# Low parts of split operands on VectorE instead of GpSimd, outside the DeltaNet's input projections

## The chip, the core and the metric

One core of a Trainium2 chip. The metric is device time in us of one execution of the kernel; the value for a kernel is the median of its runs. PE is TensorE (PEld its weight loads), DVE is VectorE, ACT is ScalarE, POOL is GpSimd, SP is SyncE, which issues most DMAs.

## What is computed

Two layers over 1040 positions (16 meta tokens and 1024 inputs) of width 1024, all in float32: the first with a gated DeltaNet as token mixer, the second with an mLSTM, each followed by a squared-ReLU MLP of width 4096.

```
for layer in range(DEPTH):                       # DEPTH = 2
    hn = rms_norm(h, attn_norm[layer])
    if layer == 0:
        mix = gated_deltanet(hn, gdn_in, gdn_conv, gdn_a_log, gdn_dt_bias, gdn_norm, gdn_out)
    else:
        mix = mlstm(hn, mlstm_in, mlstm_gate_bias, mlstm_norm, mlstm_out)
    h = h + mix
    h = h + squared_relu_mlp(rms_norm(h, ffn_norm[layer]), ff_up[layer], ff_down[layer])
return h[:, N_META:]

def squared_relu_mlp(h, w_up, w_down):
    a = jax.nn.relu(h @ w_up)
    return (a * a) @ w_down
```

The DeltaNet projects hn to queries, keys, values and gates (`gdn_in`, 6176 columns), runs a recurrence over chunks for 16 heads, and projects the result back (`gdn_out`). The mLSTM does the same with `mlstm_in` (3088 columns), 8 heads and `mlstm_out`.

## The kernel before

Every large matrix product is made from split operands. A float32 value x is written as hi + lo: hi is x rounded to the reduced-precision type that TensorE takes, made by a copy on ScalarE, and lo = x - hi, a subtraction of two SBUF tiles. `mm3` (lines 114 to 117) then issues three matmuls for each pair of tiles: hi weights with hi activations (line 115), hi weights with lo activations (116), lo weights with hi activations (117). A PSUM tile has up to 264 columns in the first layer and 504 in the last down projection.

Who makes the lo parts is the subject here:
- `load_split` (line 127) loads a block of weights into `wraw`, copies it to `whi` on ScalarE (line 134) and subtracts into `wlo` (line 135), on GpSimd unless the caller names another engine. No caller does. It is called 96 times for the DeltaNet's input projections (`GDN.load_w`), 32 for its output projection (`OutUnits.load_w`), 72 for the two down projections (`Down.tiles`), 28 for the mLSTM's input projections and 20 for its output (16 of them of 768 columns, the rest of all of 1024). Both `whi` and `wlo` have two buffers.
- `Norm.apply` (line 970 on) makes the mLSTM's normalised input; the lo parts of every second row block (8 of 16) are made by GpSimd (line 986).
- `Norm.combine` (line 989 on) makes the seven combinations of the up projection's input, for each half of the positions: 4 steps of three products and sums in SBUF (`st_b`, `st_t`, lines 1003 to 1008), then `xhi` on ScalarE and `xlo`, three of seven blocks on GpSimd (line 1011, 780 columns), four on VectorE (line 1013).
- `Up` is the up projection with seven products instead of eight for every 2 x 2 blocks (Strassen's scheme in Winograd's form). `Up.operand` makes one of the seven weight operands: sums of blocks on VectorE (line 1046), hi on ScalarE (1062), lo at line 1064. `Up.evac` adds the products up on VectorE (line 1075) and writes the activations to DRAM. A job has a flag `help`; where it is set, GpSimd makes the lo part of four of the seven operands. It is set in the first three jobs, which run on one half of the positions while `combine` still makes the other half, and in the last two, while the first activations for the down projection are loaded.

In the down projection `Down.load` splits activations on VectorE (line 1149), and each finished PSUM tile is added to the residual `hT` by VectorE (line 1168). In the DeltaNet's output projection that is line 917, from PSUM tiles with two buffers (`pj`); with it goes a square on ScalarE and its addition into `ss` on VectorE (line 941), for the next norm.

The order on each engine is set by the framework's scheduler, which takes the program's operations with their dependencies and its own estimate of their time. GpSimd also does small work of the DeltaNet and the mLSTM (powers, masks, copies), which the change leaves where it is.

Of the kernel before, what the change touches and what calls it, by code (L numbers as in the profile page):

```python
# [7 lines left out]
F32 = mybir.dt.float32  # L8
F32R = mybir.dt.float32r
AF = mybir.ActivationFunctionType  # L10
ALU = mybir.AluOpType
# [4 lines left out]
P = 128  # L16
D = 1024
KT = D // P
# [32 lines left out]
def pair(pool):  # L51
    return tuple(pool.tile([P, 2, HALF], F32R, tag=t, name="act_" + t) for t in ("hi", "lo"))
# [61 lines left out]
def mm3(nc, ps, whi, wlo, xhi, xlo, first, last):  # L114
    nc.tensor.matmul(ps, whi, xhi, start=first, stop=False)  # L115
    nc.tensor.matmul(ps, whi, xlo, start=False, stop=False)  # L116
    nc.tensor.matmul(ps, wlo, xhi, start=False, stop=last)  # L117


def staging(c, shape):  # L120
    n = 1
    for d in shape[1:]:
        n *= d
    raw = c.wraw.tile([P, 2 * HALF], F32, tag="wraw", name="wraw")[:, :n]
    return raw.rearrange("p (a b) -> p a b", a=shape[1]) if len(shape) == 3 else raw


def load_split(c, src, shape, lo_engine=None):
    nc = c.nc
    raw = staging(c, shape)  # L130
    nc.sync.dma_start(out=raw, in_=src)
    hi = c.whl.tile(shape, F32R, tag="whi", name="whi")
    lo = c.whl.tile(shape, F32R, tag="wlo", name="wlo")
    nc.scalar.copy(hi, raw)  # L134
    (lo_engine or nc.gpsimd).tensor_tensor(lo, raw, hi.bitcast(F32), op=ALU.subtract)  # L135
    return hi, lo


def rows_view(w):
    return w.rearrange("(k p) f -> p k f", p=P)  # L140
# [63 lines left out]
class GDN:  # L204
# [235 lines left out]
        yield  # L440

    def load_w(self, col):
        return load_split(self.c, rows_view(self.w)[:, :, col:col + P], [P, KT, P])

    def dense(self, whl, hf, g, m=P):
        c, n = self.c, GL[hf] // 2
# [399 lines left out]
class OutUnits:  # L846
# [17 lines left out]
    def load_w(self, k8, d):  # L864
        return load_split(self.c, rows_view(self.w)[:, 8 * k8:8 * k8 + 8, d * P:(d + 1) * P], [P, KT, P])
# [57 lines left out]
class Norm:  # L923
# [46 lines left out]
    def apply(self, hf, pool):  # L970

        nc, c = self.nc, self.c
        self.x[hf] = []
        yield
        yield
        r = yield from self.rms(hf)
        ts = slice(hf * HALF, (hf + 1) * HALF)
        for k in range(KT):
            xn = self.pool.tile([P, HALF], F32, tag="xn", name="nxn", bufs=2)
            nc.vector.scalar_tensor_tensor(xn, c.hT[:, k, ts], self.nw[:, k:k + 1],  # L980
                                           r.rearrange("p a b -> p (a b)"), op0=ALU.mult, op1=ALU.mult)
            if k % 2 == 0:
                self.x[hf].append(pair(pool))
            hi, lo = (x[:, k % 2] for x in self.x[hf][-1])
            nc.scalar.copy(hi, xn)
            (nc.vector, nc.gpsimd)[k % 2].tensor_tensor(lo, xn, hi.bitcast(F32), op=ALU.subtract)
            yield

    def combine(self, hf, pool):

        nc, c = self.nc, self.c
        self.x[hf] = []
        yield
        yield
        r = yield from self.rms(hf)
        ts = slice(hf * HALF, (hf + 1) * HALF)
        for j in range(KT // 2):
            b, t = (x.rearrange("p (a b) -> p a b", b=G) for x in self.stages())  # L1000
            hi, lo = (pool.tile([P, 7, G], F32R, tag=n, name=n) for n in ("xhi", "xlo"))
            for k, out in ((j, b[:, 0:4:3]), (j + 4, b[:, 1:3])):
                nc.vector.scalar_tensor_tensor(out, c.hT[:, k, ts].rearrange("p (a b) -> p a b", b=G),  # L1003
                                               self.nw[:, k:k + 1], r, op0=ALU.mult, op1=ALU.mult)
            nc.vector.tensor_tensor(t[:, 0], b[:, 3], b[:, 0], op=ALU.subtract)
            nc.vector.tensor_tensor(t[:, 2], b[:, 2], b[:, 3], op=ALU.subtract)
            nc.vector.tensor_tensor(t[:, 1], b[:, 2], t[:, 0], op=ALU.subtract)
            nc.vector.tensor_tensor(t[:, 3], b[:, 1], t[:, 1], op=ALU.subtract)  # L1008
            yield
            nc.scalar.copy(hi[:, 0:3], b[:, 0:3])  # L1010
            nc.gpsimd.tensor_tensor(lo[:, 0:3], b[:, 0:3], hi[:, 0:3].bitcast(F32), op=ALU.subtract)  # L1011
            nc.scalar.copy(hi[:, 3:7], t)
            nc.vector.tensor_tensor(lo[:, 3:7], t, hi[:, 3:7].bitcast(F32), op=ALU.subtract)
            self.x[hf].append((hi, lo))
            yield


class Up:
# [17 lines left out]
        nc.sync.dma_start(out=r2, in_=w[:, :, (2 * i + 1) * P:(2 * i + 2) * P])  # L1036
        return r1, r2

    def operand(self, raw, name, help):

        nc, c = self.nc, self.c
        r1, r2 = raw[:2]
        a11, a12, a21, a22 = r1[:, 0:4], r1[:, 4:8], r2[:, 0:4], r2[:, 4:8]

        def sub(out, a, b, op=ALU.subtract):
            nc.vector.tensor_tensor(out, a, b, op=op)  # L1046
            return out
        if name == "s2":
            s3 = self.u1.tile([P, KT // 2, P], F32, tag="s3", name="s3")
            raw.append(sub(s3, a11, a21))  # L1050
            x = sub(a11, a22, s3)
        elif name == "s3":
            x = raw[2]
        elif name == "s1":
            x = sub(a21, a21, a22, ALU.add)
        elif name == "s4":
            x = sub(a12, a12, a11)
        else:
            x = {"a11": a11, "a12": a12, "a22": a22}[name]
        w = c.whl.tile([P, KT, P], F32R, tag=("whi", "wlo")[self.nop % 2], name="uop")  # L1060
        self.nop += 1
        nc.scalar.copy(w[:, 0:4], x)  # L1062
        lo = nc.gpsimd if help and name in ("a12", "s3", "a22", "s4") else nc.vector
        lo.tensor_tensor(w[:, 4:8], x, w[:, 0:4].bitcast(F32), op=ALU.subtract)  # L1064
        return w

    def evac(self, i, hs, name, ps, tmp):
# [33 lines left out]
    def run(self, jobs):  # L1101

        n, ahead = len(self.ORDER), 3
        raws, ops = {0: list(self.load(jobs[0][0]))}, {}
        done = 0
        for ji, (i, parts, help, before) in enumerate(jobs):
            if before:
                before()
            hs = slice(parts[0], parts[-1] + 1)
            tmp = {}  # L1110
            for u, (name, xi) in enumerate(self.ORDER):
                while done <= min(ji * n + u + ahead, len(jobs) * n - 1):
                    dj, du = divmod(done, n)
                    ops[done] = self.operand(raws[dj], self.ORDER[du][0], jobs[dj][2])
                    if du == n - 1 and dj + 1 < len(jobs):
                        raws[dj + 1] = list(self.load(jobs[dj + 1][0]))
                    done += 1
                w = ops.pop(ji * n + u)
                ps = self.ps.tile([P, 2, 512], F32, tag="pu", name="ps_up")[:, :, :G]
                for hf in parts:  # L1120
                    for k in range(4):
                        hi, lo = (x[:, xi] for x in self.norm.x[hf][k])
                        mm3(self.nc, ps[:, hf], w[:, k], w[:, 4 + k], hi, lo, k == 0, k == 3)
                    yield
                self.evac(i, hs, name, ps[:, hs], tmp)
# [62 lines left out]
def mlp(c, w_up, w_down, norm, spans, sides, xa, st, acts, after, closed):  # L1188


    down = Down(c, w_down, acts, after, spans)
    n, e = FF // P // 2, 3
    c.norm_psum(False)
    with ExitStack() as ust:
        up = Up(c, w_up, norm, acts, ust, sides[1])
        c.bg.append(norm.combine(1, c.pool("xb", 4, ust, side=sides[1])))

        def first_done():
            xa.close()
            closed()  # L1200
            down.open(st, sides[0])
            down.fetch(0)
            for j in range(HB):
                down.load(j)
        jobs = [(i, (0,), True, None) for i in range(e)]
        for i in range(e, n - 2):
            jobs.append((i, (0, 1), False, c.drain if i == e else None))
            if i < 2 * e:
                jobs.append((i - e, (1,), False, None))
            elif i < 2 * e + 2:  # L1210
                jobs.append((n - 2 + i - 2 * e, (0,), False, None))
        jobs += [(i, (1,), True, first_done if i == n - 2 else None) for i in range(n - 2, n)]
        c.weave(up.run(jobs))
    down.open(st, sides[0])
    c.norm_psum(True)
    with ExitStack() as pst:
        down.psum = c.pool("pd", 4, pst, space=PSUM)
        c.weave(down.run())
# [538 lines left out]
```

## Time and profile before

| | us |
|---|---|
| median of 3 runs | 3264.32 (3264.29 to 3269.77) |
| profiled execution | 3269.28 |
| its span, first to last instruction | 3267.5 |
| PE busy | 3095.0 |
| DVE busy | 1910.2 |
| ACT busy | 1480.2 |
| POOL busy | 983.4 |

All later numbers of the trace come from the profiled execution. Busy times on PE are modelled and hold gaps too short to see, so the number of matmuls in a stretch says more than its busy time. The stages by time: DeltaNet 0 to 1175 (its output projection from about 1040 on, interleaved with the last scans), rest of the output projection to 1270, first up projection to 1626, first down projection to 1990, mLSTM to 2496, second output projection and up projection to 2900, second down projection to the end.

### The profile page before, as it was taken

Reading aid. Unit: us, or ns where it says so; the run is one execution under the profiler, and the core shown is the slowest. Engines: PE = TensorE matmul, PEld = TensorE weight load, DVE = VectorE, ACT = ScalarE, POOL = GpSimd, SP = SyncE. Lnnn points to the kernel's source line nnn. Section 1 sums busy time; section 2 is a strip of 40 time slices with the busy share of each in tenths; the row PEclk is TensorE's granted clock in tenths of the full one; section 3 lists DMA queues with packets and bytes.
Section 4 is the critical chain, followed back from the end, with each engine's and each line's share of the span. In section 5 each row is a group of like instructions: output and inputs, shape, how many; then the busy total and the mean of one; then the engine's idle time right before and its main releaser. Section 6 shows DMA issues by size and latency. Waiting matters only on the chain. (4 is left out here: it accounts for less than half of the span.)

```text
span 3267.5 us, 66042 instructions
## 1 busy us (share of the span) xinstructions
PE 3095.0 (95%) x26788; PEld 2933.6 (90%) x26788; DVE 1910.2 (58%) x4161; ACT 1480.2 (45%) x3394; POOL 983.4 (30%) x858
## 2 busy tenths in 40 slices
PE   7899999998999997999999998999998899999999
PEld 6888888888889897899999998988897799989998
DVE  6767778777766458776634437223237976553332
ACT  5666666665555433555511114444334555441112
POOL 4544554454444334100222224211124300022222
PEclk9899999999999998999999999999998999999999
DMA  3223223322324642433523322221122244343323
GB/s 98 75 75 88 70 80 88 88 82 76 88 67 134 206 141 73 124 120 116 161 73 98 98 66 72 60 59 51 49 91 72 82 137 123 108 132 98 104 85 97
DMA packets 402224, 311.00 MB, mean 95 GB/s; under 512 B 30175, under 2 KB 366432, under 8 KB 401920
## 3 DMA queue, kind: packets, MB, share of 16 engines
q1 hardware_dynamic: 366320, 272.69, 28.5%
q10 hardware_dynamic: 35600, 34.10, 3.0%
q8 instruction: 211, 3.46, 0.4%
q14 instruction: 93, 0.76, 0.1%
HBM read 248.11 MB, written 58.62 MB: 94 GB/s over the span
## 5 line engine op out<-in xcount | busy, mean ns | idle before, releaser
L135 POOL TENSOR_TENSOR wlo<-wraw,whi 128x1024 fp32r<-128x1024 f32 (+1 forms) x248 | 599.3, 2417 | 1163.4 <-ACT whi L134 1123.6
L115 PE MATMUL ps_up<-xhi,uop 128*128 128x260 f32 x1792 | 512.5, 286 | 27.5 <-ACT uop L1062 8.8
L115 PE MATMUL ps_dn<-act_hi,whi 128*128 128x260 f32 (+1 forms) x1792 | 534.7, 299 | 1.8 <-DVE hT L1168 1.6
L116 PE MATMUL ps_dn<-act_lo,whi 128*128 128x260 f32 (+1 forms) x1792 | 534.6, 298 | 0.0
L117 PE MATMUL ps_dn<-act_hi,wlo 128*128 128x260 f32 (+1 forms) x1792 | 532.0, 298 | 0.1
L117 PE MATMUL ps_up<-xhi,uop 128*128 128x260 f32 x1792 | 510.2, 285 | 8.1 <-DVE uop L1064 7.8
L116 PE MATMUL ps_up<-xlo,uop 128*128 128x260 f32 x1792 | 511.3, 286 | 0.2 <-POOL xlo L1011 0.2
L115 PE MATMUL ps_in<-act_hi,whi 128*128 128x264 f32 (+1 forms) x1536 | 457.1, 298 | 20.2 <-ACT raw L465 12.4
L134 ACT CAST whi<-wraw 128x1024 fp32r<-128x1024 f32 (+1 forms) x248 | 255.9, 1032 | 480.2 <-PE ps_dn L116 361.6
L116 PE MATMUL ps_in<-act_lo,whi 128*128 128x264 f32 (+1 forms) x1536 | 453.0, 295 | 0.0
L1168 DVE TENSOR_TENSOR hT<-hT,ps_dn 128x260 f32<-128x260 f32 (+1 forms) x448 | 204.8, 461 | 424.1 <-PE ps_dn L117 423.7
L117 PE MATMUL ps_in<-act_hi,wlo 128*128 128x264 f32 (+1 forms) x1536 | 451.1, 294 | 0.0
L115 PEld LDWEIGHTS ps_up<-xhi,uop 128*128 128x128 f32 x1792 | 342.6, 191 | 31.9 <-ACT uop L1062 12.5
L117 PEld LDWEIGHTS ps_up<-xhi,uop 128*128 128x128 f32 x1792 | 342.2, 191 | 9.6 <-DVE uop L1064 8.8
L115 PEld LDWEIGHTS ps_dn<-act_hi,whi 128*128 128x128 f32 x1792 | 336.9, 188 | 13.8 <-issue 1.4
L117 PEld LDWEIGHTS ps_dn<-act_hi,wlo 128*128 128x128 f32 x1792 | 337.4, 189 | 11.0 <-POOL wlo L135 0.3
L116 PEld LDWEIGHTS ps_dn<-act_lo,whi 128*128 128x128 f32 x1792 | 337.1, 188 | 10.4
L116 PEld LDWEIGHTS ps_up<-xlo,uop 128*128 128x128 f32 x1792 | 342.6, 191 | 0.5 <-POOL xlo L1011 0.4
L115 PEld LDWEIGHTS ps_in<-act_hi,whi 128*128 128x128 f32 x1536 | 294.5, 192 | 26.3 <-ACT raw L465 14.1
L117 PEld LDWEIGHTS ps_in<-act_hi,wlo 128*128 128x128 f32 x1536 | 294.5, 192 | 4.3 <-issue 1.6
L116 PEld LDWEIGHTS ps_in<-act_lo,whi 128*128 128x128 f32 x1536 | 294.6, 192 | 3.8 <-issue 1.4
L115 PE MATMUL ps_m<-act_hi,whi 128*128 128x260 f32 x768 | 224.2, 292 | 6.8 <-ACT mso L1444 3.7
(419 smaller groups left out, 6845.3 us busy)
## 6 DMA issues: line engine op xcount, KB each, us to landing
wraw<-in_gdn_in_dram SPq DMA_DIRECT2D x96, 512.0 KB
wraw<-in_ff_down_dram SPq DMA_DIRECT2D x72, 512.0 KB
a_st<-d_a SPq DMA_DIRECT2D x64, 520.0 KB
d_a<-up_c ACTq DMA_DIRECT2D x88, 260.0 KB
wraw<-in_ff_up_dram SPq DMA_DIRECT2D x42, 512.0 KB
r<-in_ff_up_dram SPq DMA_DIRECT2D x42, 512.0 KB
wraw<-in_gdn_out_dram SPq DMA_DIRECT2D x32, 512.0 KB
wraw<-in_mlstm_in_dram SPq DMA_DIRECT2D x28, 512.0 KB
```

The source lines that it names most:

```text
L115: nc.tensor.matmul(ps, whi, xhi, start=first, stop=False)
L116: nc.tensor.matmul(ps, whi, xlo, start=False, stop=False)
L117: nc.tensor.matmul(ps, wlo, xhi, start=False, stop=last)
L134: nc.scalar.copy(hi, raw)
L135: (lo_engine or nc.gpsimd).tensor_tensor(lo, raw, hi.bitcast(F32), op=ALU.subtract)
L1168: nc.vector.tensor_tensor(hT[:, d, t0:t0 + n], hT[:, d, t0:t0 + n], ps, op=ALU.add)
```

## The change

`load_split` makes `wlo` on VectorE unless told otherwise, and `GDN.load_w` now names GpSimd. `apply` and `combine` make all lo parts on VectorE, and so does `Up.operand`; the `help` flag is gone from the jobs.

```
@@ load_split
-    (lo_engine or nc.gpsimd).tensor_tensor(lo, raw, hi.bitcast(F32), op=ALU.subtract)
+    (lo_engine or nc.vector).tensor_tensor(lo, raw, hi.bitcast(F32), op=ALU.subtract)
@@ GDN.load_w
-        return load_split(self.c, rows_view(self.w)[:, :, col:col + P], [P, KT, P])
+        return load_split(self.c, rows_view(self.w)[:, :, col:col + P], [P, KT, P], self.nc.gpsimd)
@@ Norm.apply
-            (nc.vector, nc.gpsimd)[k % 2].tensor_tensor(lo, xn, hi.bitcast(F32), op=ALU.subtract)
+            nc.vector.tensor_tensor(lo, xn, hi.bitcast(F32), op=ALU.subtract)
@@ Norm.combine
-            nc.gpsimd.tensor_tensor(lo[:, 0:3], b[:, 0:3], hi[:, 0:3].bitcast(F32), op=ALU.subtract)
+            nc.vector.tensor_tensor(lo[:, 0:3], b[:, 0:3], hi[:, 0:3].bitcast(F32), op=ALU.subtract)
@@ Up.operand
-        lo = nc.gpsimd if help and name in ("a12", "s3", "a22", "s4") else nc.vector
-        lo.tensor_tensor(w[:, 4:8], x, w[:, 0:4].bitcast(F32), op=ALU.subtract)
+        nc.vector.tensor_tensor(w[:, 4:8], x, w[:, 0:4].bitcast(F32), op=ALU.subtract)
@@ mlp
-        jobs = [(i, (0,), True, None) for i in range(e)]
+        jobs = [(i, (0,), None) for i in range(e)]
...
-        jobs += [(i, (1,), True, first_done if i == n - 2 else None) for i in range(n - 2, n)]
+        jobs += [(i, (1,), first_done if i == n - 2 else None) for i in range(n - 2, n)]
```

Lines after 1063 have numbers one lower in the changed kernel. The scheduler's order is the same on all engines up to the end of the DeltaNet's scans (about 1035 us of the trace) and is made anew from there.

First place: VectorE, the end of the DeltaNet's output projection, one step of `combine` with the residual additions (`hT`, 917) and the sums of squares (`ss`, 941). Before:

```order
L1003 SCALAR_TENSOR_TENSOR st_b<-hT,ncols,nr 128x2x260
L1003 SCALAR_TENSOR_TENSOR st_b<-hT,ncols,nr 128x520
L917 TENSOR_TENSOR hT<-hT,ps_out 128x260
L1005 TENSOR_TENSOR st_t<-st_b 128x260
L1006 TENSOR_TENSOR st_t<-st_b 128x260
L917 TENSOR_TENSOR hT<-hT,ps_out 128x260
L1007 TENSOR_TENSOR st_t<-st_b,st_t 128x260
L941 TENSOR_TENSOR ss<-ss,nsq 128x260
L1008 TENSOR_TENSOR st_t<-st_b,st_t 128x260
L941 TENSOR_TENSOR ss<-ss,nsq 128x260
```

Now, at the same place:

```order
L1003 SCALAR_TENSOR_TENSOR st_b<-hT,ncols,nr 128x2x260
L1003 SCALAR_TENSOR_TENSOR st_b<-hT,ncols,nr 128x520
L1013 TENSOR_TENSOR xlo<-st_t,xhi 128x1040
L941 TENSOR_TENSOR ss<-ss,nsq 128x260
L917 TENSOR_TENSOR hT<-hT,ps_out 128x260
L1011 TENSOR_TENSOR xlo<-st_b,xhi 128x780
L1005 TENSOR_TENSOR st_t<-st_b 128x260
L1006 TENSOR_TENSOR st_t<-st_b 128x260
L917 TENSOR_TENSOR hT<-hT,ps_out 128x260
L135 TENSOR_TENSOR wlo<-wraw,whi 128x1024
```

An `xlo` of 780 columns and a `wlo` of 1024 have come into the row, between two residual additions each.

Second place: VectorE, the first down projection, residual additions (`hT`) and splits of the activations (`act_lo`). Before:

```order
L1168 TENSOR_TENSOR hT<-hT,ps_dn 128x260 x32
L1149 TENSOR_TENSOR act_lo<-a_st,act_hi 128x1040 x2
L1168 TENSOR_TENSOR hT<-hT,ps_dn 128x260 x4
L1149 TENSOR_TENSOR act_lo<-a_st,act_hi 128x1040
L1168 TENSOR_TENSOR hT<-hT,ps_dn 128x260
L1149 TENSOR_TENSOR act_lo<-a_st,act_hi 128x1040
L1168 TENSOR_TENSOR hT<-hT,ps_dn 128x260 x27
```

Now:

```order
L135 TENSOR_TENSOR wlo<-wraw,whi 128x1024
L1167 TENSOR_TENSOR hT<-hT,ps_dn 128x260 x8
L1148 TENSOR_TENSOR act_lo<-a_st,act_hi 128x1040 x2
L1167 TENSOR_TENSOR hT<-hT,ps_dn 128x260
L135 TENSOR_TENSOR wlo<-wraw,whi 128x1024
L1167 TENSOR_TENSOR hT<-hT,ps_dn 128x260 x3
L1148 TENSOR_TENSOR act_lo<-a_st,act_hi 128x1040
```

One `wlo` stands among every eight residual additions.

## Rows read from the trace of the kernel before

**Rows 1.** The page's first line.
```profile
span 3267.5 us, 66042 instructions
```
**Rows 2.** Busy time by stage; columns: stage, length, busy (instructions) by engine, clock, DMA.
```profile
core 0: us, PE busy (x) PEld busy (x) DVE busy (x) ACT busy (x) POOL busy (x), PEclk, DMA share, GB/s
...
1030.00:1175.00 145.00, 135.22 (x1309) 127.33 (x1308) 67.81 (x175) 60.44 (x149) 54.36 (x47) 0.99 0.63 197
1175.00:1220.00 45.00, 45.00 (x384) 44.94 (x384) 27.60 (x32) 16.79 (x27) 19.45 (x8) 1.00 0.29 86
1220.00:1276.00 56.00, 46.63 (x352) 45.55 (x350) 44.50 (x58) 19.47 (x31) 23.76 (x11) 0.91 0.23 66
1276.00:1340.00 64.00, 47.42 (x337) 45.23 (x337) 56.51 (x82) 32.69 (x65) 25.53 (x15) 0.92 0.29 87
1340.00:1590.00 250.00, 249.68 (x2089) 249.48 (x2088) 167.17 (x272) 135.89 (x241) 0.00 (x0) 1.00 0.40 121
1590.00:1626.00 36.00, 33.42 (x262) 32.79 (x261) 28.96 (x41) 25.99 (x46) 16.38 (x12) 0.95 0.67 205
1626.00:1955.00 329.00, 329.00 (x2750) 329.00 (x2749) 125.59 (x255) 57.76 (x59) 74.94 (x30) 1.00 0.28 88
1955.00:2035.00 80.00, 69.80 (x545) 66.76 (x543) 63.24 (x83) 33.53 (x68) 35.87 (x19) 0.96 0.24 67
...
2496.00:2530.00 34.00, 25.52 (x192) 24.21 (x191) 32.87 (x38) 11.75 (x14) 19.07 (x10) 0.94 0.23 70
2530.00:2606.00 76.00, 62.78 (x444) 59.06 (x444) 71.83 (x114) 39.67 (x84) 30.84 (x17) 0.91 0.24 70
```
**Rows 3.** Groups by line and shape, GpSimd; busy us, mean ns, idle before.
```profile
L135 POOL TENSOR_TENSOR wlo<-wraw,whi 128x1024 fp32r<-128x1024 f32 x232 | 569.0, 2453 | 1085.5 <-ACT whi L134 1067.8 <-PE ps_fin L1271 4.4 <-ACT LP L680 3.6
```
**Rows 4.** Order of time, GpSimd and VectorE; columns: start us, duration us, instruction.
```profile
1199.24 2.40 POOL L135 TENSOR_TENSOR wlo<-wraw,whi 128x1024 fp32r<-128x1024 f32 x1 [3.34 <-ACT whi L134]
...
1199.51 2.41 DVE L941 TENSOR_TENSOR ss<-ss,nsq 128x260 f32<-128x260 f32 x1 [0.90 <-ACT nsq L940]
...
1202.81 0.43 DVE L941 TENSOR_TENSOR ss<-ss,nsq 128x260 f32<-128x260 f32 x1 [0.55 <-ACT nsq L940]
```
**Rows 5.** Order of time, GpSimd and VectorE, first down projection.
```profile
1648.59 2.39 POOL L135 TENSOR_TENSOR wlo<-wraw,whi 128x1024 fp32r<-128x1024 f32 x1 [9.10 <-ACT whi L134]
...
1648.97 0.42 DVE L1168 TENSOR_TENSOR hT<-hT,ps_dn 128x260 f32<-128x260 f32 x1 [1.00 <-PE ps_dn L117]
```
**Rows 6.** Order of time, VectorE, back-to-back starts at 1252 and 1282.
```profile
1252.14 1.24 DVE L1013 TENSOR_TENSOR xlo<-st_t,xhi 128x1040 fp32r<-128x1040 f32 x1
1253.30 0.42 DVE L941 TENSOR_TENSOR ss<-ss,nsq 128x260 f32<-128x260 f32 x1
...
1281.88 0.68 DVE L1064 TENSOR_TENSOR uop<-r,uop 128x512 fp32r<-128x512 f32 x1
1282.48 0.68 DVE L1064 TENSOR_TENSOR uop<-wraw,uop 128x512 fp32r<-128x512 f32 x1
```
**Rows 7.** Order of time, VectorE, first and last prolonged instruction of three stages.
```profile
1224.76 2.63 DVE L1005 TENSOR_TENSOR st_t<-st_b 128x260 f32<-128x260 f32 x1
...
1326.08 2.17 DVE L1046 TENSOR_TENSOR wraw<-r,s 128x512 f32<-128x512 f32 x1
...
1960.66 2.36 DVE L941 TENSOR_TENSOR ss<-ss,nsq 128x260 f32<-128x260 f32 x1 [0.55 <-ACT nsq L940]
...
2031.09 2.89 DVE L980 SCALAR_TENSOR_TENSOR nxn<-hT,ncols,nr 128x520 f32<-128x520 f32 x1 [1.39 <-POOL act_lo L986]
...
2496.13 2.84 DVE L1003 SCALAR_TENSOR_TENSOR st_b<-hT,ncols,nr 128x520 f32<-128x520 f32 x2 [0.64 <-ACT nr L967]
...
2599.92 1.99 DVE L1008 TENSOR_TENSOR st_t<-st_b,st_t 128x260 f32<-128x260 f32 x1
```
**Rows 8.** Waits; columns: waiting line, releaser, us in total, times, longest.
```profile
POOL wlo L135 <- ACT whi L134: 1123.6, 209, 18.1
```

More of the change, by code (lines that the diff above doesn't have):

```diff
@@ L1037, in load, with operand @@
         return r1, r2
-    def operand(self, raw, name, help):
+    def operand(self, raw, name):
         nc, c = self.nc, self.c
@@ L1105, in run @@
         done = 0
-        for ji, (i, parts, help, before) in enumerate(jobs):
+        for ji, (i, parts, before) in enumerate(jobs):
             if before:
@@ L1113, in run @@
                     dj, du = divmod(done, n)
-                    ops[done] = self.operand(raws[dj], self.ORDER[du][0], jobs[dj][2])
+                    ops[done] = self.operand(raws[dj], self.ORDER[du][0])
                     if du == n - 1 and dj + 1 < len(jobs):
@@ L1204, in first_done @@
                 down.load(j)
-        jobs = [(i, (0,), True, None) for i in range(e)]
+        jobs = [(i, (0,), None) for i in range(e)]
         for i in range(e, n - 2):
-            jobs.append((i, (0, 1), False, c.drain if i == e else None))
+            jobs.append((i, (0, 1), c.drain if i == e else None))
             if i < 2 * e:
-                jobs.append((i - e, (1,), False, None))
+                jobs.append((i - e, (1,), None))
             elif i < 2 * e + 2:
-                jobs.append((n - 2 + i - 2 * e, (0,), False, None))
-        jobs += [(i, (1,), True, first_done if i == n - 2 else None) for i in range(n - 2, n)]
+                jobs.append((n - 2 + i - 2 * e, (0,), None))
+        jobs += [(i, (1,), first_done if i == n - 2 else None) for i in range(n - 2, n)]
         c.weave(up.run(jobs))
```

## The prediction

> **What bounds the kernel now.** I read the stage table first, then the GpSimd groups, then the order of time on VectorE and GpSimd in the slow stages. The span is 3267.5 us [rows 1]. The middle of an up projection shows TensorE at its limit: 2089 matmuls in 250 us, 8.36 in a us, clock 1.00 (from 1340 on, [rows 2]). I use that rate as the yardstick. The down projection keeps it (2750 in 329 us from 1626 on, [rows 2]), so nothing that VectorE does there matters while it stays hidden. Three stages fall far below it [rows 2]:
> - S1, 1220 to 1340, the end of the DeltaNet's output projection and the first three jobs of the up projection, with `combine` beside both: 352 + 337 = 689 matmuls, 82.4 us at the full rate, in 120 us. 37.6 us are lost.
> - S2, 1955 to 2035, end of the first down projection with `apply`: 545 matmuls, 65.2 us in 80. 14.8 us are lost.
> - S3, 2496 to 2606, S1 again in the second layer: 192 + 444 = 636, 76.1 us in 110. 33.9 us are lost.
> In each, VectorE is the busy engine: 101 of 120 us, 63 of 80, 105 of 110. [...]
>
> Why VectorE is so busy is seen in the order of time. At 1199.24 GpSimd starts a `wlo` that takes 2.40 us; VectorE's `ss` addition at 1199.51, 260 columns out of SBUF, takes 2.41 us, though the same line takes 0.43 us at 1202.81, with GpSimd idle [rows 4]. The VectorE instruction lasts until the GpSimd one is over. An addition with one input in PSUM isn't held: `hT` at 1648.97 takes 0.42 us inside a `wlo` of GpSimd that runs from 1648.59 for 2.39 us [rows 5]. So VectorE's busy time in S1 to S3 is partly waiting for GpSimd.
>
> [...]
>
> **The change, part by part.** 216 GpSimd instructions go to VectorE: 152 of line 135 (32 output projection of the DeltaNet, 72 down projections, 48 mLSTM), 16 of line 1011, 40 of line 1064, 8 of line 986. The 96 `wlo` of the DeltaNet's input projections stay, in a unit that GpSimd needs 2.45 us for [rows 3].
>
> What one costs on VectorE: an instruction over 1040 columns starts 1.16 us before the next, one over 512 columns 0.60 us (1252.14 to 1253.30, 1281.88 to 1282.48 [rows 6]). On the line through these two: 1.14 us for 1024 columns, 0.88 for 780, 0.87 for 768, 0.61 for 520.
>
> What it gives back: I took each SBUF-to-SBUF instruction of VectorE in S1 to S3 that is longer than the same shape with GpSimd idle, and summed the excess; [rows 7] has the first and the last of each stage.
> - S1: 22 instructions, 31.8 us of excess. Added: 5 `wlo` of 1024, 8 of 780, 12 of 512, so 5.7 + 7.0 + 7.2 = 19.9 us. Net relief 11.9 us.
> - S3: 25 instructions, 32.1 us. Added: 3 of 768, 2 of 1024, 8 of 780, 12 of 512, 19.1 us. Net relief 13.0 us.
> - S2: 16 instructions, 24.7 us. Added: 10 of 1024 and 8 of 520, 16.3 us. Net relief 8.4 us.
> Since VectorE is busy nearly throughout S1 and S3 and TensorE has far less to do, I take the net relief there as time won, 24.9 us; the bounds are nothing and all that TensorE loses, 71.5 us. S2 begins with TensorE still near full speed, so only the later part can pay: I take 5 us (bounds 0 and 8.4).
>
> The end of each up projection (1590 to 1626, and the same code in the second layer) had GpSimd's help on purpose: 8 lo parts of 512 columns and the first `wlo`, 8 x 0.60 + 1.14 = 5.9 us more on VectorE, which is already busy 29 of 36 us while TensorE loses 36 - 262 / 8.36 = 4.7 us [rows 2]. Little is held up there, so this is a cost: I take 1.75 us each, 3.5 together (bounds 0 and 11.8).
>
> The rest I cost at nothing. The down projections: about 70 `wlo`, one for 8 evictions in the new order; TensorE covers them, since a tile of 8 evictions lasts 96 matmuls, 11.5 us, and VectorE is busy 126 of 329 us [rows 2]. If a `wlo` came too late there, each would cost up to 1.14 us. The mLSTM's projections: their PSUM is emptied by ScalarE, VectorE is lightly used. The DeltaNet's tail (1030 to 1175): 16 `wlo`, 18 us more on VectorE, which idles 77 of 145 us there while TensorE is busy 135 [rows 2]; but the scheduler orders the last scan and the first output units anew, so I keep 4 us of gain to 8 us of loss. Before that point the order is the same row for row. GpSimd's own remaining work gets shorter queues, which I count as nothing.
>
> Sum: 11.9 + 13.0 + 5 - 3.5 = 26.4 us. The profiled execution took 3269.28 us, of which 3267.5 are the span; it lies 5.0 us above the median of 3264.32. So 3269.3 - 26.4 = 3242.9 as a profiled execution, and 3237.9 as a median.
>
> [...]
>
> **Rivals.**
> *The feed is the bound, not VectorE's time.* TensorE needs hi from ScalarE, then lo, then matmuls, and in S1 VectorE idles 19 of 120 us while TensorE loses 37.6: half of the loss has another cause. If the relief only turns into VectorE waiting for ScalarE and for weights, a quarter of the 33.3 us of net relief is won, 8 us, less the 3.5 of the tails: 3260. Against it: in S3 VectorE idles only 5 of 110 us.
> *TensorE recovers its clock too.* [...] If half of the 86.3 us lost in the three stages comes back: 3221. For it: clock 0.91 in 1220 to 1276 and in 2530 to 2606. Against it: `combine`'s own VectorE work stays.
> *Slower: VectorE stands before a lo part.* GpSimd waited 1123.6 us for ScalarE's `whi`, 209 times, 5.4 us each [rows 8]; nobody stood behind it. VectorE takes its instructions in order, and behind a `wlo` that waits stand the evictions. In the two output projections, 52 `wlo` with PSUM in two banks of 24 matmuls (2.9 us) each in the DeltaNet's. It decides from about half a us of lost TensorE time per `wlo` on: that eats the 26 us. At 1 us each it is 52 - 26.4 = 26 us slower, 3290. Against it: `whi` is ready about 1 us after the tile changes, and the new order sets `wlo` between evictions.
>
> **How the numbers follow.** Likeliest, net relief in S1 to S3: 0.64, 3238. Clock and feed too: 0.15, 3221. Feed-bound: 0.12, 3260. VectorE held up: 0.09, 3290. The first two are faster by over 0.2% (6.5 us, about what a measurement of this kernel can tell from no change), so faster 0.79; the third counts as the same, 0.12; slower 0.09. The range goes to below the second case, and on the other side just past the third: 3215 to 3262; what it leaves out is the held-up case and the ends of the unknown costs.
>
> **What would show it.** Right: in the profile after, the `ss` and `st_t` additions of 260 columns at 0.42 us everywhere beyond the DeltaNet's input projections, S1 and S3 shorter by 10 to 15 us each, with as many matmuls and a higher clock; VectorE's busy time up by clearly less than the 200-odd us that moved; down projections at 8.36 matmuls in a us. Wrong: TensorE waiting for `wlo` or for `hT` behind a `wlo` in the output projections; gaps in the down projections; ends of the up projections longer by several us; a longer DeltaNet tail; or S1 and S3 as long as before with VectorE idle.

## The result: 46 us faster, and the profile after

The changed kernel takes 3219.15 us (median of 4 runs, 3217.56 to 3221.43) against 3265.16 us (3264.29 to 3269.77) for the kernel before: a ratio of 0.9857, 95% interval 0.984 to 0.9874. That is a gain of 46 us. The forecast was 3238, a gain of 26. So sign and range held, and the size was too small by 20 us.

The page of the changed kernel, its first lines (busy us, share of the span, instructions):

```profile
span 3217.2 us, 65599 instructions
...
PE 3086.3 (96%) x26788; PEld 2924.8 (91%) x26788; DVE 1991.4 (62%) x4377; ACT 1483.3 (46%) x3394; POOL 507.8 (16%) x642
```

GpSimd lost 476 us of busy time. VectorE got 216 instructions more, over 200 us of work by the prices of the prediction, and its busy time rose by only 81 us (from 1910.2). The rest is additions that are no longer held. Two groups of the kernel before and then of the changed one show it (VectorE's additions into `ss`, all 84; columns: busy us, mean ns, idle before):

```profile
L941 DVE TENSOR_TENSOR ss<-ss,nsq 128x260 f32<-128x260 f32 x84 | 69.0, 829 | 23.1 <-ACT nsq L940 22.8
```
```profile
L941 DVE TENSOR_TENSOR ss<-ss,nsq 128x260 f32<-128x260 f32 x84 | 35.1, 424 | 8.6 <-ACT nsq L940 8.0
```

The same instructions take half: 424 ns instead of 829, as [rows 4] showed one by one.

Now the stages. I cut the trace of the changed kernel where as many matmuls had started as at the cuts of [rows 2], so each row below answers to a row there (columns as there; at the first cut, which falls into a burst of small matmuls, the counts differ by some 20):

```profile
1026.60:1165.40 138.80, 133.49 (x1332) 125.44 (x1321) 77.38 (x194) 64.13 (x162) 19.16 (x34) 1.00 0.65 206
...
1210.20:1255.10 44.90, 41.92 (x352) 41.45 (x350) 38.25 (x71) 21.63 (x38) 0.00 (x0) 1.00 0.28 83
1255.10:1309.20 54.10, 46.29 (x336) 44.29 (x337) 50.07 (x93) 31.30 (x60) 0.00 (x0) 0.94 0.31 92
...
1600.80:1931.30 330.50, 329.61 (x2750) 329.41 (x2749) 158.17 (x287) 57.61 (x61) 0.00 (x0) 1.00 0.27 87
1931.30:2000.20 68.90, 67.75 (x545) 66.78 (x544) 54.20 (x99) 34.40 (x67) 0.10 (x1) 0.95 0.29 85
...
2462.00:2484.80 22.80, 22.80 (x192) 22.80 (x191) 21.98 (x40) 9.97 (x12) 0.00 (x0) 1.00 0.31 98
2484.80:2557.60 72.80, 60.40 (x444) 55.37 (x443) 69.77 (x138) 41.99 (x87) 0.00 (x0) 0.98 0.26 76
```

Against [rows 2]: the end of the DeltaNet 145 to 138.8 us, S1 120 to 99.0 (352 and 336 matmuls as before, in 44.9 and 54.1), S2 80 to 68.9, S3 110 to 95.6. S1's first part reads best: VectorE does 71 instructions in 38 us where it did 58 in 44.5, and the granted clock is 1.00 instead of 0.91. With the moved instructions counted in, VectorE's busy time fell by 12.7 us in S1 (101.0 to 88.3), by 13.0 in S3 (104.7 to 91.8) and by 9.0 in S2 (63.2 to 54.2): the net relief that the prediction worked out (11.9, 13.0 and 8.4) came nearly to the us. The down projection is nearly as it was (329.0 to 330.5 us), with 32 more instructions on VectorE.

The order of the two kernels parts at about 1006 us, not at the 1035 given with the change: VectorE's first `wlo` of the output projection stands at 1007.07. Up to there the traces differ by 0.3 us. From there to the 1030 us point the kernel before takes 22.9 us and the changed one 19.3. Most of that is not the change: a run below that keeps the order of before until 1209 us (the one with four PSUM buffers) takes 20.0 us for the same 245 matmuls, at a granted clock of 1.00 like the changed kernel, where the profiled execution of before had 0.85. Of the 50.3 us between the spans, 47 stand behind the 1030 us point.

### The profile page after: what moved, and what is told of

Same layout as the page of the kernel before. It is cut to its first block, busy times and chain, and to the rows that moved or that the text cites. A ratio compares the mean times of both kernels' runs of the same rounds, so it can differ in the third digit from the quotient of the medians.

```text
span 3217.2 us, 65599 instructions
## 1 busy us (share of the span) xinstructions
PE 3086.3 (96%) x26788; PEld 2924.8 (91%) x26788; DVE 1991.4 (62%) x4377; ACT 1483.3 (46%) x3394; POOL 507.8 (16%) x642
## 4 chain that ended last, share of the span: by engine, by line
PE 68%; DVE 20%; ACT 5%; DMA 4%; issue 2%; POOL 0%; POOLq 0%; SPq 0%; ACTq 0%; DVEq 0%
PE ps_dn L115 7%; PE ps_dn L116 7%; PE ps_dn L117 7%; PE ps_up L115 6%; PE ps_up L116 6%; PE ps_up L117 5%; DVE acc L473 3%; PE ps_m L115 3%; PE ps_m L116 3%; PE ps_m L117 3%; DVE acc L471 2%; DVE tm L622 2%; PE ps_out L115 2%; PE ps_out L116 2%; PE ps_out L117 2%
## 5 line engine op out<-in xcount | busy, mean ns | idle before, releaser
L115 PE MATMUL ps_in<-act_hi,whi 128*128 128x264 f32 (+1 forms) x1536 | 458.3, 299 | 18.6 <-ACT raw L465 12.1
L135 POOL TENSOR_TENSOR wlo<-wraw,whi 128x1024 fp32r<-128x1024 f32 x96 | 230.2, 2398 | 172.0 <-ACT whi L134 160.1
L135 DVE TENSOR_TENSOR wlo<-wraw,whi 128x1024 fp32r<-128x1024 f32 (+1 forms) x152 | 181.8, 1196 | 97.5 <-ACT whi L134 96.7
```

The source lines that it names most:

```text
L135: (lo_engine or nc.vector).tensor_tensor(lo, raw, hi.bitcast(F32), op=ALU.subtract)
```

## The experiments

Theory, as in the prediction (*hold*, in some expectations "lock theory"): a GpSimd instruction that reads SBUF holds VectorE instructions that read SBUF, and in S1 to S3 VectorE's time is the kernel's. Main rival (*ready earlier*): a lo part is simply ready sooner on VectorE (1.2 us instead of 2.4, no queue of GpSimd), and so are the weights and the buffers behind it. The table has the length in us of the stretches with equal matmul counts, from the traces of the runs:

| | before | after | weights only | norms only | GpSimd spare | VectorE spare |
|---|---|---|---|---|---|---|
| DeltaNet's end (1030 to 1175) | 145.0 | 138.8 | 138.2 | 144.7 | 138.5 | 138.3 |
| S1 (1220 to 1340) | 120.0 | 99.0 | 105.1 | 107.2 | 134.9 | 132.0 |
| 1340 to 1590 | 250.1 | 253.2 | 250.1 | 251.4 | 249.9 | 249.9 |
| S2 (1955 to 2035) | 80.2 | 69.0 | 71.7 | 79.7 | 74.4 | 73.4 |
| S3 (2496 to 2606) | 110.0 | 95.6 | 99.7 | 96.3 | 119.8 | 115.4 |
| median of the kernel | 3265 | 3219 | 3229 | 3243 | 3289 | 3279 |

**One half of the change each.** The kernel before, with line 135 alone on VectorE (and `GDN.load_w` on GpSimd):

```
-    (lo_engine or nc.gpsimd).tensor_tensor(lo, raw, hi.bitcast(F32), op=ALU.subtract)
+    (lo_engine or nc.vector).tensor_tensor(lo, raw, hi.bitcast(F32), op=ALU.subtract)
```

> Only the 152 weight lo parts go to VectorE; the 64 lo parts of the norms and of the up projection's operands stay on GpSimd. Net relief by the trace of before, split by which GpSimd instruction the prolonged VectorE instruction ended with: S1 8 us of excess against 5.7 us added, S2 16 against 11.4, S3 10 against 4.9, so a gain of 12 us from these, plus the 6 us that the end of the DeltaNet gained: about 18 of the 46 us, 3246. If the gain came from the operands being ready earlier (a weight lo part takes 1.2 us on VectorE and 2.4 on GpSimd), weights carry most of it: 3230 or less. If the two halves get in each other's way (VectorE stands behind the rest of GpSimd's work with more on its list), no gain: 3260 or more.

And the other half, the changed kernel with the weights back on GpSimd:

```
-    (lo_engine or nc.vector).tensor_tensor(lo, raw, hi.bitcast(F32), op=ALU.subtract)
+    (lo_engine or nc.gpsimd).tensor_tensor(lo, raw, hi.bitcast(F32), op=ALU.subtract)
```

> Only the 64 lo parts of the norms and of the up projection's operands go to VectorE; all weight lo parts of load_split stay on GpSimd. Net relief theory: S1 24 us of excess against 14.2 added, S2 8 against 4.9, S3 22 against 14.2, less the ends of the up projections: a gain of some 18 to 21 us, 3245; the 6 us at the end of the DeltaNet stay lost. Together with the run with only the weights it should make up the 46 us, within 8 us. Operands-ready-earlier theory: little gain, 3258.

Measured: 3228.98 (0.9882, 0.9867 to 0.9896) and 3243.04 (0.9922, 0.9907 to 0.9937), gains of 37 and 23 us. The norms' half came as worked out, the weights' half twice as large: all of the DeltaNet's end, 8.5 of the 11.3 us of S2, 15 in S1 where net relief gave 2.3. Together they make 60, not 46 (the forecast was 46 within 8): in S1 and S3 the halves gain partly the same microseconds. Taken alone, the first run speaks for *ready earlier* (3230 or less), the second against it (it asked for 3258). The trace of the kernel before speaks against it too: in the whole kernel TensorE waits 3.3 us for lo parts that GpSimd makes, 2.8 of them for `wlo`. The longest entry (us in total, times, longest):

```profile
PE ps_out L117 <- POOL wlo L135: 1.6, 2, 1.4
```

In the changed kernel it waits for no `wlo`. A late lo part could still act through the buffers behind it, so a run is needed.

**GpSimd's instructions back, the lo parts as they are.** The changed kernel, and beside the lo parts of the weights from the last quarter of the DeltaNet's output projection on (in S2 and S3 those around the norm), of `combine`, of every second block of `apply`, and of the operands in the first three and last two jobs:

```
+        c.nc.gpsimd.tensor_tensor(out, x, x, op=ALU.add)
```

Here x is the lo part, or a half of it, and out a spare tile.

> The changed kernel, and beside it GpSimd adds each of the moved lo parts to itself into a spare tile that nobody reads (8 weight blocks at the end of the DeltaNet's output projection, all 16 blocks of combine, the 40 operands, the last 13 or so weight blocks around the norm in S2 and its 8 lo parts, 4 weight blocks in S3). Nothing waits for these. If what cost time was GpSimd reading SBUF while VectorE adds out of SBUF, the excess is back in S1, S2 and S3 (some 30, 25 and 30 us) on top of the work that VectorE now does itself: 40 to 80 us slower than the changed kernel, 3260 to 3300. If the gain came from operands that are ready earlier, from the new order or from queues, GpSimd's extra work costs nothing: 3215 to 3225.

The same with `c.nc.vector` in place of `c.nc.gpsimd`:

> The same spare additions, made by VectorE instead of GpSimd: they are 24 us of VectorE work in S1, some 15 in S2, 19 in S3 and 5 at the end of each up projection (0.60 us for 512 columns, 0.34 for 260). If VectorE's time in these stages is time of the kernel one to one, as the sum assumed, this costs 50 to 65 us, 3270 to 3285. If it is worth half, 30 us: 3250. If VectorE's time is not the limit, under 10 us.

Measured: 3288.82 (1.006, 1.0045 to 1.0075) and 3278.97 (1.0035, 1.0024 to 1.0046): 70 and 60 us slower than the changed kernel. In the run with GpSimd's additions every lo part is still made by VectorE, without GpSimd's queue. The two stretches of S1 in it (columns as in [rows 2]):

```profile
1210.90:1275.20 64.30, 46.36 (x353) 45.15 (x351) 48.43 (x72) 22.29 (x38) 25.28 (x22) 0.86 0.20 58
1275.20:1345.70 70.50, 50.72 (x336) 48.16 (x337) 62.69 (x96) 32.59 (x62) 26.76 (x19) 0.81 0.27 80
```

In the first row VectorE is busy 48.4 us with 72 instructions, where 71 took 38.3 in the changed kernel, and the clock falls to 0.81 to 0.86. That is the hold; GpSimd's queue, the cause in *ready earlier*, is not in it. Late lo parts are, as a consequence: VectorE, held, comes to them later, and TensorE waits 16.0 us for its `wlo`, 9.9 of them in S1. (The spare additions also keep `wlo` buffers for longer; VectorE waits 9.0 us for that in the whole kernel, a small part of 70.) With VectorE's own spare additions, S1 has 40 of them, 25.7 us by their durations, and with the stretch behind it is 29.7 us longer (132.0 + 249.9 against 99.0 + 253.2); S3 has 36, 22.2 us, and is 19.8 us longer (18.3 with the stretch behind it); S2 has 23, 15.8 us, and is 4.4 us longer. So VectorE's time is worth some 1.15 us of the kernel in S1, 0.8 to 0.9 in S3, and 0.3 in S2.

**Which instructions it takes.** The kernel before, with the 32 weight lo parts of the DeltaNet's output projection on VectorE (`OutUnits.load_w`):

```
-        return load_split(..., [P, KT, P])
+        return load_split(..., [P, KT, P], self.nc.vector)
```

> The kernel before, with one thing changed: the 32 weight lo parts of the DeltaNet's output projection are made on VectorE. By the ledger of equal matmul counts of the runs with only the weights and only the norms' parts, the end of the DeltaNet (6.3 us) and most of what the weights give in S1 (14 us of its 15) come from these 32 instructions: some 20 us, 3246. If weights elsewhere (down projection, mLSTM) carry it through the order, under 8 us: 3258 or more.

Measured: 3242.54 (0.9928, 0.9911 to 0.9944), 22 us. The DeltaNet's end takes 138.5 us and S1 107.2, S2 and S3 81.0 and 110.4 as before. 32 of 216 instructions carry nearly half of the gain.

The changed kernel, with the 72 of the down projections back on GpSimd (`Down.tiles`):

```
-            "(h p) f -> p h f", p=P), [P, HB, 256])
+            "(h p) f -> p h f", p=P), [P, HB, 256], nc.gpsimd)
```

> The changed kernel with the 72 weight lo parts of the down projections back on GpSimd. Their residual additions read PSUM and weren't prolonged, so the full stretch of the down projections stays as it is (within 2 us of 329); what comes back is the part that runs beside the norm in S2, 8 of them: S2 69 to 75 us, so 3219 to 3226. If the 82 us of VectorE work that they take had cost anything, it would be faster than the changed kernel: 3210.

Measured: 3224.00 (0.987, 0.9855 to 0.9885). The down projection takes 330.4 us against 330.5 with them on VectorE, and S2 75.0 against 69.0; the whole kernel is 4.9 us slower than the changed one, with intervals that overlap. Nothing in the full stretch, 6 us where the norm runs beside it.

The changed kernel, with GpSimd's four operands of seven back in the last two jobs alone:

```
+        lo = nc.gpsimd if help and name in ("a12", "s3", "a22", "s4") else nc.vector
...
+                    ops[done] = self.operand(raws[dj], self.ORDER[du][0], dj >= len(jobs) - 2)
```

> The changed kernel with GpSimd's help back in the last two jobs of each up projection alone (16 lo parts of operands). By the sum that help was worth 3.5 us: 3215.7. By the ledger the two ends together cost nothing (one 2.4 us longer, one 3.2 us shorter): 3219, within 3 us. Against both: prolonged additions come back there, 3224.

Measured: 3215.05 (3209.5 to 3219.3; 0.984, 0.9824 to 0.9856), not to be told from the changed kernel, and as little from the 3215.7 of the sum. In the trace, which is of the slowest of the four runs, the two ends take 36.3 and 39.8 us, 38.4 and 36.8 without the help.

**The lo parts that the change leaves out.** The changed kernel, with the DeltaNet's input projections on VectorE too:

```
-        return load_split(..., [P, KT, P], self.nc.gpsimd)
+        return load_split(..., [P, KT, P])
```

> The changed kernel, with the 96 weight lo parts of the DeltaNet's input projections on VectorE as well: 96 x 1.14 = 109 us more there, where VectorE is busy 560 of 750 us and TensorE 706. Lock theory: VectorE's additions out of SBUF are no longer prolonged there either, but TensorE is covered for most of it; 10 us faster to 10 us slower than the changed kernel, 3209 to 3229. VectorE's time is the limit in the scans: 30 us or more slower, 3250. Weights ready earlier, as at the output projection: 10 us or more faster, 3209 or less.

Measured: 3127.28 (0.9569, 0.9555 to 0.9584), 92 us faster than the changed kernel and 137 faster than before: the best version here. Its VectorE is busy 1940.6 us, 51 less than in the changed kernel, with 96 instructions more. Of the three forecasts only that of *ready earlier* (3209 or less) fits the number; that of the hold (3209 to 3229) missed by 82 us, for it counted VectorE's additions alone. One group of VectorE shows 66 us of what is no longer held (the convolution's first product, out of SBUF with a column of factors; first the changed kernel, then this one; columns as above):

```profile
L471 DVE TENSOR_SCALAR acc<-raw,ncols 128x512 f32<-128x512 f32 x32 | 52.7, 1646 | 21.7 <-ACT raw L465 21.4
```
```profile
L471 DVE TENSOR_SCALAR acc<-raw,ncols 128x512 f32<-128x512 f32 x32 | 16.9, 528 | 0.0
```

With the 32 of 528 columns (46.8 us, then 16.2), 99.5 us have become 33.1. In order of time in the changed kernel, this instruction and a `wlo` of GpSimd start together and end together, within 0.3 us:

```profile
666.77 2.40 POOL L135 TENSOR_TENSOR wlo<-wraw,whi 128x1024 fp32r<-128x1024 f32 x1
```
```profile
666.75 2.70 DVE L471 TENSOR_SCALAR acc<-raw,ncols 128x512 f32<-128x512 f32 x1 [0.42 <-ACT raw L465]
```

Three runs on top of this one ask what it is about GpSimd. With a spare addition of each of these 96 lo parts, with as long a time of GpSimd that only writes, and with one column of each made again by GpSimd, so that TensorE needs GpSimd's queue once more (in this order; x is half of a lo part):

```
+            nc.gpsimd.tensor_tensor(scr, x, x, op=ALU.add)
...
+        nc.gpsimd.tensor_copy(scr[:, 0:1], lo[:, 0, 0:1].bitcast(F32))
+        for h in range(4):
+            nc.gpsimd.memset(scr, 0.0)
...
+        nc.gpsimd.tensor_tensor(lo[:, KT - 1, P - 1:], raw[:, KT - 1, P - 1:], hi[:, KT - 1, P - 1:].bitcast(F32),
+                                op=ALU.subtract)
```

> The kernel with all lo parts on VectorE (3127), and beside it GpSimd adds each of the 96 lo parts of the DeltaNet's input projections to itself into a spare tile that nobody reads, in two instructions of 512 columns. The lo parts are ready as early as without. Lock theory: VectorE's busy time, 160 us shorter without those GpSimd instructions, becomes as much longer again, and the 92 us are lost: 3200 to 3280. Theory that the 92 us come from weights that are ready earlier: 3125 to 3140.

> As the run with the spare additions, but GpSimd's spare work reads next to nothing: after each lo part it copies one column of it and then fills a spare tile of 512 columns four times (some 0.52 us each by the row of its memset). As long on GpSimd's queue, without reading SBUF. If it is the reading that holds VectorE: 3127 to 3155, of which the 64 TENSOR_SCALAR of the convolution may take a part. If it is GpSimd's time, through the DeltaNet's small work that stands behind in its queue: as with the spare additions, 3200 or more.

> The kernel with all lo parts on VectorE (3127), and GpSimd makes the last column of each of the 96 lo parts of the DeltaNet's input projections again: some 0.2 us of GpSimd instead of 2.45, but TensorE's third matmul waits again for GpSimd's queue to come to it. If the 92 us come from lo parts that no longer stand in GpSimd's queue behind its other work: most of them are lost, 3190 or more. Lock theory: at most a quarter is lost, 3127 to 3150.

Measured: 3191.81 (3187.74 to 3193.01), 3139.31 (3132.7 to 3148.12) and 3130.74 (3130.66 to 3132.33): 65, 12 and 3.5 us more than the 3127; the third can hardly be told from it (0.9584, 0.9568 to 0.96). GpSimd's time was alike in the first two (groups of GpSimd, of the first and of the second run; the second has 96 copies of one column besides, 26.2 us):

```profile
L453 POOL TENSOR_TENSOR scr<-wlo 128x512 f32<-128x512 f32 x192 | 221.3, 1153 | 230.8 <-DVE wlo L135 155.5 <-DVE tm L632 39.3 <-DVE sso L714 9.3
```
```profile
L452 POOL MEMSET scr<- 128x512 f32 x384 | 204.7, 533 | 19.4
```

So it is the reading, for the most part: 221 us of it cost 65 us of the kernel, 231 us of nearly only writing cost 12, and standing in GpSimd's queue, a shorter one than the changed kernel's, 3.5 at most. In the first run the trace lists no wait of VectorE for a `wlo` buffer that the spare additions keep. So some 52 to 65 of the 92 us are the hold. TensorE's waits up to the end of the DeltaNet fit: for the recurrence's state `S`, which VectorE makes, 15.7 us in the changed kernel and 1.2 with all lo parts on VectorE; for `raw`, ScalarE's copy out of PSUM, 12.1 and 2.8; for a `wlo` none in either. The first run missed its range (3200 to 3280) by 8 us: the spare additions come behind the lo part and meet other instructions of VectorE than `wlo` did (VectorE is busy 2030.5 us, 90 more, not the 160 I had put down). The other 27 to 40 us stay open.

**PSUM instead.** The weights' half gave far more in S1 than the time that they free on VectorE. In the first part of S1 TensorE waits for residual additions that would empty one of two PSUM buffers (the waits of the kernel before, 1220 to 1278.6; us, times, longest):

```profile
PE ps_out L115 <- DVE hT L917: 9.1, 4, 3.3
```

The kernel before, with four PSUM buffers for the last quarter of the output projection and nothing moved:

```
+        units.ps = c.pool("po4", 4, dst, space=PSUM)
...
-                ps = c.pj.tile([P, 512], F32, tag="pj", name="ps_out")[:, :G]
+                ps = (self.ps or c.pj).tile([P, 512], F32, tag="pj", name="ps_out")[:, :G]
```

> The kernel before, with all lo parts where they were; the last quarter of the DeltaNet's output projection gets four PSUM buffers instead of two. In 1220 to 1278.6 of before TensorE waits 9.1 us for residual additions (hT) that stand behind prolonged VectorE instructions, and its clock is 0.91. If the gain there is that additions no longer come too late for two buffers, four buffers give most of it without any lo part moved: this stretch 58.6 to 50 us or less, and 8 to 14 us in all. If VectorE's busy time as a whole is what counts (47 of 58.6 us, 54 of the next 61), the time only moves on: 0 to 4 us in all, with the next stretch as much longer.

Measured: 3256.50 against 3264.01 (0.9976, 0.9967 to 0.9985), 7.5 us, between the two. That part of S1 goes from 58.6 to 54.0, the wait from 9.1 to the following, and the next part is 1.2 us shorter, not longer:

```profile
PE ps_out L115 <- DVE hT L917: 3.7, 2, 1.9
```

Some 6 of S1's 21 us are held additions that come too late for two buffers. In the changed kernel that wait is gone. The rest of the 7.5 us does not stand in S1: S3, where this run moves nothing, is 3.5 us shorter in its trace (106.5 against 110.0), in another order. So a stage's length in a single trace can differ by some 3 us without any lo part moved.

## Why the prediction was right, and where its sum was short

**Mechanism: right.** Putting GpSimd's reading back beside unchanged lo parts costs 70 us, and VectorE's busy time rose by 81 us for over 200 us of work. The 260-column additions are at 0.42 us everywhere, S1 and S3 are shorter with as many matmuls and at a higher clock, as "What would show it" asked. For VectorE's instructions with two inputs out of SBUF it is GpSimd's reading that holds, not its fills: on average the convolution's SCALAR_TENSOR_TENSOR over 528 columns takes 0.93 us in the run with spare additions, 0.77 in that with fills and 0.77 with neither (over 512 columns 0.90, 0.76 and 0.77). Of VectorE's TENSOR_TENSOR and SCALAR_TENSOR_TENSOR that overlap nothing of GpSimd but those, 105 of 264 are longer than the same shape with GpSimd idle beside the additions (by over 0.05 us), and none of 341 beside the fills.

**The terms of the sum**, forecast and measured (gain in us, by equal matmul counts):

| term | forecast | measured |
|---|---|---|
| before 1030 | 0 | 3.4, mostly not of the change |
| DeltaNet's end | 0 (gain 4 to loss 8) | 6.3 |
| S1 | 11.9 | 21.0, of which 3.1 are given back by 1590 |
| ends of the up projections | -3.5 | -2.4 and +3.2 |
| first down projection | 0 | -1.5 |
| S2 | 5 (0 to 8.4) | 11.3 |
| mLSTM | 0 | -1.0 |
| S3 | 13.0 | 14.4, of which 1.3 are given back by 2860 |
| last down projection | 0 | 0 |

The 20 us that the sum was short are S1 (6.0 net), S2 (6.3), the DeltaNet's end (6.3) and the ends of the up projections (4.3), less 2.5 of small losses.

- *S3* came out, and the price of one to one for VectorE's time nearly holds there (0.8 to 0.9 by the run with VectorE's spare additions). Some luck is in it: its clock rose from 0.94 and 0.91 to 1.00 and 0.98, which by the working in the next point is up to 7 us, and the sum had no term for that.
- *S1* is the first term that was mis-sized: 17.9 net instead of 11.9. VectorE's time costs 1.15 us for one, and some of the held additions stood before the one that TensorE waited for: four PSUM buffers give 6 us without any relief. The clock is in it too. Where the traces have it below 1.00 for a stretch, it is 0.50: before, from 1238 to 1242, with 12 and 11 matmuls in 2 us, against 19 and 19 at 1.00 from 1244 to 1248. So at 0.91 and 0.92 some 20 us of 120 are at that level (twice the missing share, times the length), at 1.00 and 0.94 some 6.5 of 99; at half a us each, an estimate from these counts, that is up to 7 us. The runs don't tell wait and clock apart: the stretches with less waiting are those with the higher clock.
- *S2* broke its bound: 11.3 against at most 8.4. I weighed it by VectorE's busy time, which is worth only 0.3 there; nor was VectorE the busy engine of that stage, as the prediction reads it (63 us of 80, TensorE 70 [rows 2]). It is the weights' lo parts beside the norm: 8.5 us by the run with the weights alone, 6 lost again when those of the down projection go back, next to nothing by the norm's own. A chain was held, not a full engine: TensorE's waits there fall from 10.0 us to 1.1, and the largest of them is for the `ss` in front of the norm (waits in S2, before and after):

```profile
PE ps_nrm L949 <- DVE ss L941: 4.4, 3, 1.7
```
```profile
PE ps_nrm L949 <- DVE ss L941: 1.1, 1, 1.1
```

- *DeltaNet's end* also left its bounds. I kept 4 us for a new order and looked for no held instruction, since VectorE idles there; and the order is new from 1006 us on, not from 1030. But the idle VectorE stood before a late load. The kernel before, GpSimd and VectorE in order of time:

```profile
1156.21 2.37 POOL L135 TENSOR_TENSOR wlo<-wraw,whi 128x1024 fp32r<-128x1024 f32 x1 [6.49 <-ACT whi L134]
```
```profile
1157.13 2.54 DVE L861 TENSOR_TENSOR act_lo<-ost,act_hi 128x1040 fp32r<-128x1040 f32 x1 [2.51 <-ACT act_hi L860]
...
1168.92 1.24 DVE L861 TENSOR_TENSOR act_lo<-ost,act_hi 128x1040 fp32r<-128x1040 f32 x1 [6.92 <-ACT act_hi L860]
1170.08 0.42 DVE L917 TENSOR_TENSOR hT<-hT,ps_out 128x260 f32<-128x260 f32 x1
```

  The first split is held (2.54 us instead of 1.24), and at the third VectorE waits 6.9 us for its data, with a residual addition queued behind it that TensorE needs. In the changed kernel the wait at this place is 2.0 us:

```profile
1159.41 1.24 DVE L861 TENSOR_TENSOR act_lo<-ost,act_hi 128x1040 fp32r<-128x1040 f32 x1 [1.98 <-ACT act_hi L860]
```

  The 32 parts of this projection alone bring it. Whether the held split delays that load, or the staging buffer that GpSimd reads for longer, wasn't tried apart and stays open.
- *The ends of the up projections* cost nothing in the two traces, one 2.4 us longer and one 3.2 us shorter, so the sum had 3.5 us too much. The run with the help back (3215.05) does not settle it: a cost of 3.5 us is not ruled out.
- *The down projections* were right: 72 lo parts more on VectorE, 329.0 us before and 330.5 after in the first, 362.1 both times in the second.

**The rivals.** Feed-bound (3260) and VectorE held up (3290) did not come. In the changed kernel VectorE does stand before `wlo` for ScalarE's `whi` (94 us over 136 of them), but TensorE waits nowhere for a `wlo`. The rival with the clock gave 3221, nearer to the 3219 than the likeliest case, and its condition came: of the 86.3 us lost in the three stages, 46.7 come back, 42.3 without what is given back behind S1 and S3. The clock rose in S1 and S3, but not in S2 (0.96 and 0.95). The net relief came as well, in VectorE's busy time. So the range held, but the likeliest case does not stand above this rival: how much of the excess in S1 is clock and how much shorter waits stays open, and the excess in S2 and at the DeltaNet's end (granted clock 0.99 and 1.00) is not clock.

## What to carry to other kernels

Where GpSimd reads SBUF beside a busy VectorE, sum the excess of VectorE's instructions over the same shape with GpSimd idle, everywhere and not only where VectorE is full: what a held instruction cost here lay in what stood behind it, residual additions for a PSUM buffer (some 6 of S1's 21 us) or an `ss` in front of a norm (TensorE's wait 4.4 us, then 1.1), and perhaps a load. Then price VectorE's time in each stage by doubling some of its work there; it was worth 0.3 to 1.15 us for one in stages of one kernel. And look for more of the same outside the change: the 96 lo parts that it left on GpSimd were worth twice as much as the 216 that it moved.

## What was not expected of the hardware

- A VectorE instruction with a single large SBUF input can be held too: TENSOR_SCALAR over 512 columns takes 0.53 us with the weights' lo parts gone from GpSimd, less than the 0.68 of an addition of two [rows 6], and 1.65 on average in the changed kernel. The prediction's example is an addition of two tiles [rows 4].
- This kind is held by GpSimd's fills as well, only for less long (a fill takes 0.53 us). On average the convolution's TENSOR_SCALAR takes only 0.52 us over 512 columns and 0.54 over 528 in the run with the fills, because few meet one. Where it meets nothing of GpSimd but fills, all 6 take longer, 0.56 to 0.79 us against 0.48 to 0.49 with GpSimd idle; of all TENSOR_SCALAR, 23 of 28. So for this kind writing is not free, and part of the 12 us that the fills cost may be a hold. The longest of the 6 starts 0.02 us after the first of two fills:

```profile
380.56 1.28 POOL L452 MEMSET scr<- 128x512 f32 x2
```
```profile
380.58 0.79 DVE L480 TENSOR_SCALAR acc<-raw,ncols 128x528 f32<-128x528 f32 x1
```
